# A hybrid retention/mLSTM layer step: third and fourth heads swapped, conditioning rows moved from the first mixer projection to the output projection, gates one head later

## The chip, the core and the metric

The kernel runs on one core of a Trainium2 chip. The metric is the device time of one execution in microseconds (us). A core has TensorE (PE) for matrix products, VectorE (DVE) and ScalarE (ACT) for elementwise work, GpSimd (POOL) for some more of it, and 16 DMA engines; the SyncE queue (SP) issues nearly all loads. Each engine works off its own queue strictly in order, and instructions wait on semaphores for other engines.

## What is computed

One layer over 384 tokens of width 2048 (128 context tokens and 256 latent tokens): adaptive layer norm, a mixer of four retention heads and four mLSTM heads, an output projection with a residual and post-norm, then a convolutional feed-forward block.

```python
sh1, sc1, g1, sh2, sc2, g2 = jnp.split(silu(c) @ w_mod + b_mod, 6)   # conditioning, context and latent
h = _ln(x) * (1.0 + sc1) + sh1
proj = h @ w_in                       # per head q, k, v and an output gate; 16 gate columns
gates = proj[..., off + 4 * M:] + b_gate        # input and forget gates of the mLSTM heads
ret_out = _ln(retention forward + backward) * gn_ret * silu(rg)       # 4 heads of 256
mlstm_out = sigmoid(mo) * _ln(mlstm forward + backward) * gn_mlstm    # 4 heads of 256
x = _ln(ALPHA * x + g1 * (concat(ret_out, mlstm_out) @ w_out)) * ln1_g + ln1_b
h = _ln(x) * (1.0 + sc2) + sh2
x = _ln(ALPHA * x + g2 * ffn(h)) * ln2_g + ln2_b
```

## The kernel before

Every large product is made to float32 accuracy out of three TensorE passes: a weight tile `raw` is split into a high part `hi` (ScalarE, line 117) and a low part `lo` (mostly VectorE, every sixth tile on GpSimd, line 118), and the products hi·hi, hi·lo and lo·hi are added up (lines 182 to 184 and 190 to 192). There are four `raw` buffers and three each of `hi` and `lo`, so a split can run at most about three weight tiles ahead of TensorE.

The mixer works head by head. Heads 0 and 1 of the retention are projected in a first phase, while the first parts of the conditioning are computed. The remaining six heads stand in the list `heads` at positions 2 to 7 (retention 2 and 3, mLSTM 0 to 3), and a loop over these positions projects each: `proj_a` for q and k (`psa`, four weight tiles each) and `proj_b` for v and the output gate (`psb`, eight weight tiles), so 16 weight tiles a head. After each weight tile `beside()` lets three generators go on by a number of steps that their `rate` sets:

- `behind`: the attention of the head two positions earlier (at position 7, of those at 5 and 6). Its products are `sc` (scores), `pm` (mLSTM decay rows), `num` (outputs), `cst_ps` or `rst_ps` (new states) and `mxp` (transposes into the rows `mixt`).
- `gating`, rate 0.5: the mLSTM gates (`cps`, `gsum`, `gsel`, `gcp` on TensorE; logarithms, scans and copies on VectorE, lines 547 to 555 and 594 to 642).
- `mods2`, rate 0.9: five blocks of conditioning rows. A block takes 16 loads `mraw` of 512 KB from `w_mod` (three buffers), two VectorE multiply-adds into `macc` for each (lines 283 and 286, so 32 a block), then TensorE sums over partitions (`modr`), the bias is added (`mbt`) and the row goes to memory. There is one `macc` buffer.

After the loop the first 512 columns of the output projection are begun (`pso`, seven weight tiles beside the attention of position 7), and finished with the two last rows of `mixt`, which that attention delivers; then come the other three column blocks.

The order in which the code is written only gives priorities: the framework's scheduler lists the instructions by its own timeline, and an instruction written later may stand earlier when its inputs are ready. PSUM tiles of the attentions, of the gates and of `modr` share three buffers (`pat`).

In what follows S2 to S7 are the stretches in which positions 2 to 7 are projected, and O is the one of the first output columns. Each begins with the first matmul of its `psa` (or `pso`) in TensorE's timeline.

Of the kernel before, what the change touches and what calls it, by code (L numbers as in the profile page):

```python
# [17 lines left out]
KT = D // P  # L18
# [5 lines left out]
NH = 4  # L24
# [58 lines left out]
def hybrid_step(ctx, tc, ca, cb, x_prompt, x_sample, state_ret, state_c, state_n, state_m, c, c_ctx,  # L83
# [29 lines left out]
    def transpose(out, in_, n=P):  # L113
        nc.tensor.transpose(out, in_, ident[:n, :n])
# [20 lines left out]
    def rows_bcast(dst, src_row, n):  # L135
        nc.gpsimd.dma_start(out=dst, in_=src_row.to_broadcast([P, n]))

    def weights(loads, n=1024, perm=False):
        raw = wraw.tile([P, 1024], F32, tag="raw", name="raw")
        for view, src in loads:  # L140
            nc.sync.dma_start(out=view(raw), in_=src)
        return split_weights(raw, n, perm)
# [19 lines left out]
    def weights_b(w2, k0, nk, cols):  # L162
        n = 512 // len(cols)
        loads = []
        for j, c0 in enumerate(cols):
            src = w2[k0 * P:(k0 + nk) * P, c0:c0 + n].rearrange("(k p) n -> p k n", p=P)
            loads.append((lambda r, j=j: r[:, :nk * 512].rearrange("p (k n) -> p k n", k=nk)[:, :, j * n:(j + 1) * n],
                          src))
        return weights(loads, nk * 512)
# [4 lines left out]
    def new_act(kt, src, eng=None):  # L174
        act_hi[kt] = acts.tile([P, T], F32R, tag=f"ah{kt}", name=f"ah{kt}")
        act_lo[kt] = acts.tile([P, T], F32R, tag=f"al{kt}", name=f"al{kt}")
        split(act_hi[kt], act_lo[kt], src, eng)
# [8 lines left out]
    def mm_b(ps, w, kk, ah, al, tt, start, stop, c0=0, n=512):  # L186
        hi, lo = w
        s = slice(kk * 512 + c0, kk * 512 + c0 + n)
        t = slice(tt * P, (tt + 1) * P)
        nc.tensor.matmul(ps, lhsT=ah[:, t], rhs=hi[:, s], start=start, stop=False)  # L190
        nc.tensor.matmul(ps, lhsT=ah[:, t], rhs=lo[:, s], start=False, stop=False)  # L191
        nc.tensor.matmul(ps, lhsT=al[:, t], rhs=hi[:, s], start=False, stop=stop)  # L192
# [3 lines left out]
    def rstd(out, var, n=1):  # L196
        v = small.tile([P, NT], F32, tag="veps", name="veps")
        nc.vector.tensor_scalar(out=v[:, :n], in0=var, scalar1=EPS, scalar2=None, op0=ALU.add)
        with tc.high_priority():
            mark["pow"] = nc.gpsimd.tensor_tensor(out=out, in0=v[:, :n], in1=mhalf[:, :n], op=ALU.pow).ins  # L200
# [118 lines left out]
    def chain(*gens):  # L319
        for g in gens:  # L320
            yield from g
# [66 lines left out]
    def part_b(ps, w, nk, k0, ks, ke):  # L388
        for kk in range(nk):
            kt = k0 + kk  # L390
            for tt in range(NT):
                mm_b(ps[tt], w, kk, act_hi[kt], act_lo[kt], tt, kt == ks, kt == ke)
# [26 lines left out]
    with ExitStack() as p0:  # L419
# [53 lines left out]
        for kt in range(KT):  # L473
            ps = pmm.tile([P, T], F32, tag="ps", name="xtp")
# [40 lines left out]
    with p1:  # L515
# [72 lines left out]
        def gates():  # L588
# [49 lines left out]
            for n, src in enumerate((ga, gem)):  # L638
                for d in range(2):
                    for tt in range(NT):  # L640
# [4 lines left out]
        gating = Stepper(gates(), 0.5)  # L645
# [3 lines left out]
        mods2 = Stepper(chain(mod_vector(2, pat, mp, raws2), mod_vector(3, pat, mp, raws2),  # L649
                              mod_vector(4, pat, mp, raws2, range(NV))), 0.9)  # L650
# [47 lines left out]
        def head_tail(hh, og, gn, h, last=False):  # L698
            st = small.tile([P, NT, 6], F32, tag="hst", name="hst")
            mv = small.tile([P, NT, 2], F32, tag="hmv", name="hmv")  # L700
            rs = small.tile([P, NT], F32, tag="hrs", name="hrs")
            for tt in range(NT):
                nc.vector.bn_stats(out=st[:, tt, :], in_=hh[:, tt, :])
                nc.vector.bn_aggr(out=mv[:, tt, :], in_=st[:, tt:tt + 1, :])
            rstd(rs, mv[:, :, 1], NT)
            for tt in range(NT):
                nc.vector.tensor_scalar(out=hh[:, tt, :], in0=hh[:, tt, :], scalar1=mv[:, tt, 0:1],
                                        scalar2=rs[:, tt:tt + 1], op0=ALU.subtract, op1=ALU.mult)
            g = gn[:, h * HD:(h + 1) * HD].unsqueeze(1).to_broadcast([P, NT, HD])
            if last:  # L710
                nc.vector.tensor_tensor(og, og, g, op=ALU.mult)
            else:
                nc.gpsimd.tensor_tensor(out=og, in0=og, in1=g, op=ALU.mult)
            nc.vector.tensor_tensor(hh, hh, og, op=ALU.mult)
# [22 lines left out]
        def mlstm_attn(h, q, k, vx, og):  # L737
# [3 lines left out]
            for d in range(2):  # L741
# [28 lines left out]
                i = d * 8 + h * 2  # L770
# [6 lines left out]
            hh = sb.tile([P, NT, HD], F32, tag="hh", name="hh", bufs=1)  # L777
            for tt in range(NT):
                for d in range(2):
                    ps = pat.tile([P, 257], F32, tag="ps", name="num")  # L780
# [22 lines left out]
                        nc.vector.scalar_tensor_tensor(out=hh[:, tt, :], in0=ps[:, 0:HD], scalar=dn,  # L803
                                                       in1=hh[:, tt, :], op0=ALU.mult, op1=ALU.add)
                yield
            head_tail(hh, og, gn_m[0], h, h == NH - 1)
            for d in range(2):
                st = sb.tile([P, 2, HD], F32, tag="st", name="st")
                for kd in range(2):
                    ps = pat.tile([P, 257], F32, tag="ps", name="cst_ps")  # L810
# [3 lines left out]
                    i = d * 8 + h * 2 + kd  # L814
# [21 lines left out]
        def ret_attn(h, q, k, vx, og):  # L836
# [62 lines left out]
            for fd in range(2):  # L899
                mix_columns(hh, 2 * h, fd)  # L900
                yield

        heads = [(ret_proj, ret_attn, h) for h in range(NH)] + [(mlstm_proj, mlstm_attn, h) for h in range(NH)]
        got = list(first)
        gn_m = []

        def attention(i):
            return heads[i][1](heads[i][2], *got[i])

        def new_acts(*kts):  # L910
            for kt in kts:
                new_act(kt, mixt[kt])

        for i in range(2, 8):
            if i == 6:
                gating.finish()
                gn_m.append(tab.tile([P, 1024], F32, tag="gn", name="gnm"))
                rows_bcast(gn_m[0], gn_mlstm.rearrange("a h v -> a (h v)"), 1024)
            last = i == 7
            behind[:] = [Stepper(chain(*[attention(j) for j in ((5, 6) if last else (i - 2,))]), 1.55 if last else 1.0)]  # L920
            got.append(heads[i][0](heads[i][2], [lambda j=j: new_acts(2 * j, 2 * j + 1) for j in range(5)] if last else ()))
            behind.pop().finish()
        mods2.finish()
        new_acts(*range(10, KT - 2))
        wo = w_out[0]
        pso = [pmm.tile([P, 512], F32, tag="ps", name="pso") for _ in range(NT)]
        attn = Stepper(attention(7), 1.75)
        attn.step()
        for k0 in range(0, KT - 2, 2):
            part_b(pso, weights_b(wo, k0, 2, (0,)), 2, k0, 0, KT - 1)  # L930
            attn.step()
        attn.finish()
        pn = pat.tile([16, P], F32, tag="ps", name="pn")
        transpose(pn, ncol)
        nrow = tab.tile([16, P], F32, name="nrow")
# [46 lines left out]
    with ExitStack() as p2:  # L982
# [2 lines left out]
        g1b = g1p.tile([P, 2, D], F32, name="g1b")  # L985
        l1g = g1p.tile([P, D], F32, name="l1g")
        l1b = g1p.tile([P, D], F32, name="l1b")
        for kt in range(KT - 2, KT):
            new_act(kt, mixt[kt])
        mixs.close()  # L990
        share_splits(0)
# [7 lines left out]
        def residual_loads(nb):  # L999
            s = slice(nb * 512, (nb + 1) * 512)  # L1000
            for tt in range(NT):
                nc.sync.dma_start(out=r[tt][:, s], in_=tok_rows(x_prompt, x_sample, tt)[:, s])
            for v in range(2):
                nc.sync.dma_start(out=g1b[:, v, s], in_=modrow[2, v:v + 1, s].to_broadcast([P, 512]))

        def w_out_block(nb):
            ps = pso if nb == 0 else [(pat if nb == 1 else pmm).tile([P, 512], F32, tag="ps", name="pso")
                                      for _ in range(NT)]
            for k0 in range(KT - 2 if nb == 0 else 0, KT, 2):
                part_b(ps, weights_b(wo, k0, 2, (nb * 512,)), 2, k0, 0, KT - 1)  # L1010
                if nb > 0:
                    mods4.step()
                if k0 == (10 if nb else KT - 2):
                    residual_loads(nb)
                if nb == 2 and k0 == 14:
                    residual_loads(3)
                if nb == 1 and k0 == 8:
                    mod_from_rows(3, KT, pat, sb2, "sh2", 0.0)
                if nb == 2 and k0 == 6:
                    rows_bcast(l1g, ln1_g, D)  # L1020
                    rows_bcast(l1b, ln1_b, D)
                if nb == 2 and k0 == 8:
                    mod_from_rows(4, 8 * NV, pat, sb2, "sc2", 1.0)
            return ps

        for nb in range(3):
            ps = w_out_block(nb)
            for tt in range(NT):
                residual(sb2, g1b, tt, nb, ps[tt], True, True)
# [3 lines left out]
        ps = [pmm.tile([P, 512], F32, tag="ps", name="pso") for _ in range(NT)]  # L1033
# [67 lines left out]
        for i in range(KT + 2):  # L1101
# [6 lines left out]
            kt = i - 2  # L1108
# [109 lines left out]
    for nb in range(4):  # L1218
        for k0 in (39, 41):
# [3 lines left out]
            i = len(ws)  # L1223
# [58 lines left out]
```

## Time and profile before

| | us |
|---|---|
| median of 3 runs (2072.29 to 2074.78) | 2074.51 |
| the profiled execution | 2073.23 |
| its span, first to last instruction | 2071.4 |
| TensorE busy in the span | 1989.1 (96%) |
| VectorE busy | 1231.2 (59%) |
| ScalarE busy | 690.3 (33%) |
| GpSimd busy | 238.4 (12%) |
| S2 to S7 and O, 227.4 to 814.9 | 587.5 |

Busy time of TensorE is that of overlapping records, so a stretch without idle time may still hold matmuls that are paced by a lower clock; the granted clock is listed beside it. A number in square brackets behind a row of a timeline is the idle time of the engine just before it, with the instruction that ended it.

### The profile page before, as it was taken

The numbers are of one execution on the slowest core, as the hardware profiler recorded it, in microseconds if no ns is written. First come the engines' busy times: TensorE is split into PE (matmuls) and PEld (weight loads), VectorE is DVE, ScalarE is ACT, GpSimd is POOL, SyncE is SP. The second block draws the span as 40 slices with busy tenths as digits, with TensorE's granted clock in tenths as the row PEclk, the third lists the DMA queues.
The fourth block names the chain that finished last, engine by engine and source line by source line (L and its number), as shares of the span: only waits on it lengthen the run. The fifth ranks groups of instructions, "written<-read, shape, count | busy, mean of one in ns | idle before, by whom it ended". The sixth has DMA issues, their size and how long they took to land.

```text
span 2071.4 us, 26316 instructions
## 1 busy us (share of the span) xinstructions
PE 1989.1 (96%) x10233; PEld 1752.3 (85%) x10233; DVE 1231.2 (59%) x1791; ACT 690.3 (33%) x1050; POOL 238.4 (12%) x226
## 2 busy tenths in 40 slices
PE   6999899999989999998999999999999999999995
PEld 4677878899888876777999889999889998999984
DVE  4655699987868754477944333477434444444478
ACT  4223333333333443235333333333222332233331
POOL 0001353231212111012000000000000000000004
PEclk9999999999999999998999999999999999999998
DMA  9895976887886435834744334466334444434342
GB/s 346 259 308 167 167 189 182 257 211 214 199 175 213 147 111 209 282 109 140 251 124 125 125 127 123 125 193 195 123 122 126 125 136 153 123 110 143 113 153 102
DMA packets 260637, 352.30 MB, mean 170 GB/s; under 512 B 16143, under 2 KB 200784, under 8 KB 259360
## 3 DMA queue, kind: packets, MB, share of 16 engines
q1 hardware_dynamic: 256240, 340.08, 55.3%
q0 software_dynamic: 4272, 10.54, 1.5%
q8 instruction: 80, 1.31, 0.3%
q14 instruction: 45, 0.37, 0.1%
HBM read 343.16 MB, written 7.41 MB: 169 GB/s over the span
## 4 chain that ended last, share of the span: by engine, by line
PE 81%; DVE 7%; DMA 5%; issue 3%; POOL 1%; SPq 1%; ACT 1%; POOLq 0%; DVEq 0%; ACTq 0%
PE psu L182 11%; PE psu L184 11%; PE psu L183 11%; PE psd L192 5%; PE psd L190 5%; PE psd L191 5%; PE psa L182 3%; PE psa L184 3%; PE psa L183 3%; DMA mraw<-in_w_mod 3%; PE psb L191 3%; DVE macc L286 3%; PE psb L192 3%; PE psb L190 3%; PE pso L190 2%
## 5 line engine op out<-in xcount | busy, mean ns | idle before, releaser
L118 DVE TENSOR_TENSOR lo<-raw,hi 128x1024 fp32r<-128x1024 f32 (+4 forms) x443 | 479.9, 1090 | 541.6 <-ACT hi L117 541.2
L117 ACT CAST hi<-raw 128x1024 fp32r<-128x1024 f32 (+4 forms) x473 | 435.1, 929 | 977.9 <-PE psu L183 358.8
L183 PE MATMUL psu<-al,hi 128*128 128x384 f32 x1376 | 467.4, 340 | 0.0
L184 PE MATMUL psu<-ah,lo 128*128 128x384 f32 x1376 | 464.1, 339 | 2.7 <-DVE lo L118 2.7
L182 PE MATMUL psu<-ah,hi 128*128 128x384 f32 x1376 | 466.6, 340 | 0.0
L286 DVE SCALAR_TENSOR_TENSOR macc<-mraw,ct,macc 128x1024 f32<-128x1024 f32 x210 | 287.6, 1405 | 17.4 <-DMA mraw<-in_w_mod 17.4
L184 PEld LDWEIGHTS psu<-ah,lo 128*128 128x128 f32 x1376 | 258.9, 188 | 3.0 <-DVE lo L118 3.0
L182 PEld LDWEIGHTS psu<-ah,hi 128*128 128x128 f32 x1376 | 258.8, 188 | 1.9 <-ACT hi L117 0.8
L183 PEld LDWEIGHTS psu<-al,hi 128*128 128x128 f32 x1376 | 259.2, 188 | 0.1
L192 PE MATMUL psd<-hi,fal 128*128 128x512 f32 (+1 forms) x484 | 191.3, 395 | 0.0
L191 PE MATMUL psd<-lo,fah 128*128 128x512 f32 (+1 forms) x484 | 189.5, 392 | 0.0
L190 PE MATMUL psd<-hi,fah 128*128 128x512 f32 (+1 forms) x484 | 187.7, 392 | 0.0
L184 PE MATMUL psa<-ah,lo 128*128 128x384 f32 x512 | 176.9, 347 | 7.5 <-DVE lo L118 7.4
L182 PE MATMUL psa<-ah,hi 128*128 128x384 f32 x512 | 179.7, 356 | 1.7 <-ACT hi L117 1.7
L183 PE MATMUL psa<-al,hi 128*128 128x384 f32 x512 | 176.9, 346 | 0.0
L191 PE MATMUL psb<-lo,ah 128*128 128x512 f32 x384 | 155.2, 404 | 5.5 <-DVE lo L118 5.5
L192 PE MATMUL psb<-hi,al 128*128 128x512 f32 x384 | 153.5, 400 | 0.0
L190 PE MATMUL psb<-hi,ah 128*128 128x512 f32 x384 | 151.7, 408 | 1.7 <-ACT hi L117 1.7
L182 PEld LDWEIGHTS psa<-ah,hi 128*128 128x128 f32 x512 | 98.1, 192 | 15.5 <-issue 8.8
L191 PEld LDWEIGHTS psd<-lo,fah 128*128 128x128 f32 x484 | 90.8, 188 | 22.4
L192 PEld LDWEIGHTS psd<-hi,fal 128*128 128x128 f32 x484 | 90.9, 188 | 21.6
L190 PEld LDWEIGHTS psd<-hi,fah 128*128 128x128 f32 x484 | 90.9, 188 | 20.9
(301 smaller groups left out, 2240.7 us busy)
## 6 DMA issues: line engine op xcount, KB each, us to landing
raw<-in_w_up SPq DMA_DIRECT2D x168, 512.0 KB, 3.8
mraw<-in_w_mod SPq DMA_DIRECT2D x112, 512.0 KB, 5.0
raw<-in_w_down SPq DMA_DIRECT2D x84, 512.0 KB, 3.6
raw<-in_w_in SPq DMA_DIRECT2D x128, 256.0 KB, 4.6
raw<-in_w_in SPq DMA_DIRECT2D x52, 512.0 KB, 6.7
wm<-in_w_mod SPq DMA_DIRECT2D x20, 1024.0 KB, 8.9
raw<-in_w_out SPq DMA_DIRECT2D x32, 512.0 KB, 4.0
wm<-in_w_mod SPq DMA_DIRECT2D x16, 768.0 KB, 7.4
```

Source lines behind the costliest of these rows:

```text
L117: nc.scalar.copy(dst_hi, src)
L118: mark["lo"] = (eng or nc.vector).tensor_tensor(out=dst_lo, in0=src, in1=dst_hi.bitcast(F32), op=ALU.subtract).ins
L182: nc.tensor.matmul(ps, lhsT=hi[:, s], rhs=ah, start=start, stop=False)
L183: nc.tensor.matmul(ps, lhsT=hi[:, s], rhs=al, start=False, stop=False)
L184: nc.tensor.matmul(ps, lhsT=lo[:, s], rhs=ah, start=False, stop=stop)
L190: nc.tensor.matmul(ps, lhsT=ah[:, t], rhs=hi[:, s], start=start, stop=False)
L191: nc.tensor.matmul(ps, lhsT=ah[:, t], rhs=lo[:, s], start=False, stop=False)
L192: nc.tensor.matmul(ps, lhsT=al[:, t], rhs=hi[:, s], start=False, stop=stop)
L286: nc.vector.scalar_tensor_tensor(out=acc[:, v, :], in0=raw, scalar=ct[:, kt, v:v + 1], in1=acc[:, v, :], op0=ALU.mult, op1=ALU.add)
```

## The change

Three things are changed. The heads stand in the order 0, 1, 3, 2 for both kinds, so that the last head to be attended writes rows 12 and 13 of `mixt`, and the output projection leaves these two for last. The rate of `mods2` is 0 at position 2 and 0.94 from position 3 on, and what is left of it steps on beside the seven weight tiles of O. The rate of `gating` is 0.6 at position 3 and 0 elsewhere.

```diff
-            head_tail(hh, og, gn_m[0], h, h == NH - 1)
+            head_tail(hh, og, gn_m[0], h, h == turn[-1])
...
-        heads = [(ret_proj, ret_attn, h) for h in range(NH)] + [(mlstm_proj, mlstm_attn, h) for h in range(NH)]
+        turn = (0, 1, 3, 2)
+        heads = [(ret_proj, ret_attn, h) for h in turn] + [(mlstm_proj, mlstm_attn, h) for h in turn]
...
         for i in range(2, 8):
+            mods2.rate = 0.0 if i == 2 else 0.94
+            gating.rate = 0.6 if i == 3 else 0.0
...
-        mods2.finish()
-        new_acts(*range(10, KT - 2))
+        new_acts(10, 11, 14, 15)
...
-        for k0 in range(0, KT - 2, 2):
-            part_b(pso, weights_b(wo, k0, 2, (0,)), 2, k0, 0, KT - 1)
+        for k0 in (0, 2, 4, 6, 8, 10, 14):
+            part_b(pso, weights_b(wo, k0, 2, (0,)), 2, k0, 0, 13)
+            mods2.step()
             attn.step()
         attn.finish()
+        mods2.finish()
...
-        for kt in range(KT - 2, KT):
+        for kt in (12, 13):
             new_act(kt, mixt[kt])
...
-            for k0 in range(KT - 2 if nb == 0 else 0, KT, 2):
-                part_b(ps, weights_b(wo, k0, 2, (nb * 512,)), 2, k0, 0, KT - 1)
+            for k0 in (12,) if nb == 0 else range(0, KT, 2):
+                part_b(ps, weights_b(wo, k0, 2, (nb * 512,)), 2, k0, 0, KT - 1 if nb else 13)
```

What the scheduler makes of it is seen in the order of the instructions.

First, VectorE near the start of S2. `macc<-mraw` are the conditioning rows, `lo<-raw` halves of split weight tiles, `rt` and `k` the rotation of the keys of the first two heads, `tz` the decay table of an attention. Before:

```order
L840 SCALAR_TENSOR_TENSOR tz<-cs,lgb_2129,tz 128x384
L283 TENSOR_SCALAR macc<-mraw,ct 128x1024 x2
L843 TENSOR_TENSOR tz<-tz,cst 128x128
L286 SCALAR_TENSOR_TENSOR macc<-mraw,ct,macc 128x1024 x2
L118 TENSOR_TENSOR lo<-raw,hi 128x4x128
L844 TENSOR_SCALAR tz<-tz 128x384
L567 TENSOR_TENSOR rt_2148<-k,cs 128x256
L118 TENSOR_TENSOR lo<-raw,hi 128x4x128
```

The same place after:

```order
L840 SCALAR_TENSOR_TENSOR tz<-cs,lgb_2129,tz 128x384
L843 TENSOR_TENSOR tz<-tz,cst 128x128
L844 TENSOR_SCALAR tz<-tz 128x384
L118 TENSOR_TENSOR lo<-raw,hi 128x4x128
L567 TENSOR_TENSOR rt_2148<-k,cs 128x256
L118 TENSOR_TENSOR lo<-raw,hi 128x4x128
L568 TENSOR_TENSOR rt_2149<-k,cs 128x256
L570 TENSOR_TENSOR k<-k,cs 128x256
L569 TENSOR_TENSOR k<-k,cs 128x256
L283 TENSOR_SCALAR macc<-mraw,ct 128x1024 x2
```

The first rows of `macc` no longer stand ahead of this weight tile. They have not left S2, though: all 32 of the first block still stand on VectorE ahead of the first weight tile of S3, since nothing before them there keeps them back. What does leave S2 are the gates. The first block's `modr`, which before came in S3, now comes in S4, and with one `macc` buffer no `macc` stands in S3 at all. The last block's last 14 `macc` and its `modr` stand in O.

Second, VectorE in S6, where the attention of the first mLSTM head begins (`wt<-pm` are its decay weights). Before:

```order
L286 SCALAR_TENSOR_TENSOR macc<-mraw,ct,macc 128x1024 x6
L118 TENSOR_TENSOR lo<-raw,hi 128x1024
L286 SCALAR_TENSOR_TENSOR macc<-mraw,ct,macc 128x1024 x2
L118 TENSOR_TENSOR lo<-raw,hi 128x1024
L286 SCALAR_TENSOR_TENSOR macc<-mraw,ct,macc 128x1024 x3
L751 TENSOR_TENSOR wt_4998<-pm,cs 128x256
L751 TENSOR_TENSOR wt_4998<-pm,cs 128x128 x2
L286 SCALAR_TENSOR_TENSOR macc<-mraw,ct,macc 128x1024
```

After, at the same attention:

```order
L286 SCALAR_TENSOR_TENSOR macc<-mraw,ct,macc 128x1024 x4
L118 TENSOR_TENSOR lo<-raw,hi 128x1024 x2
L751 TENSOR_TENSOR wt_4932<-pm,cs 128x256
L751 TENSOR_TENSOR wt_4932<-pm,cs 128x128 x2
L118 TENSOR_TENSOR lo<-raw,hi 128x1024
L763 SCALAR_TENSOR_TENSOR wt_4932<-sc_4890,wt_4932 128x256
```

The `macc` right ahead of and among the `wt` are gone. Instead ten `macc` of the next block stand further on in S6, between the first and the second `hh` that adds both directions of this attention. In S7 likewise no `macc` stands any more among the `wt` of the attention of position 5.

Third, TensorE in O, at the second `pm` of the last attention (that of position 7). Before, 32 rows of `pso` stand between it and its `num`:

```order
L192 MATMUL pso<-hi,al_6496 128x512
L190 MATMUL pso<-hi,ah_6508 128x512
L191 MATMUL pso<-lo,ah_6508 128x512
L192 MATMUL pso<-hi,al_6509 128x512
L743 MATMUL pm<-gnegm,cst 128x384
L190 MATMUL pso<-hi,ah_6508 128x512
L191 MATMUL pso<-lo,ah_6508 128x512
L192 MATMUL pso<-hi,al_6509 128x512
```

After:

```order
L190 MATMUL pso<-hi,ah_6494 128x512
L191 MATMUL pso<-lo,ah_6494 128x512
L192 MATMUL pso<-hi,al_6495 128x512
L743 MATMUL pm<-gnegm,cst 128x384
L795 MATMUL num<-vx,wt_6541 128x257
L795 MATMUL num<-vx,wt_6565 128x257
L795 MATMUL num<-vx,wt_6541 128x257
L795 MATMUL num<-c_6560,qs 128x257 x2
```

The `num` of the last attention now follow its second `pm` at once. Those of the attention before it, which before stood at the end of S7, stand in O, and the last attention's `sc` come after three quarters of O's `pso`. The orders of the feed-forward block and of what follows it differ by little.

More of the change, by code (lines that the diff above doesn't have):

```diff
@@ L1008, in w_out_block @@
                                       for _ in range(NT)]
-            for k0 in range(KT - 2 if nb == 0 else 0, KT, 2):
-                part_b(ps, weights_b(wo, k0, 2, (nb * 512,)), 2, k0, 0, KT - 1)
+            for k0 in (12,) if nb == 0 else range(0, KT, 2):
+                part_b(ps, weights_b(wo, k0, 2, (nb * 512,)), 2, k0, 0, KT - 1 if nb else 13)
                 if nb > 0:
                     mods4.step()
-                if k0 == (10 if nb else KT - 2):
+                if k0 == (10 if nb else 12):
                     residual_loads(nb)
```

## The prediction

> **What bounds the kernel now.** I read the page's busy times and chain first, then busy times by stage, then in each stage the waits of TensorE.
>
> ```profile
> span 2071.4 us, 26316 instructions
> PE 1989.1 (96%) x10233; PEld 1752.3 (85%) x10233; DVE 1231.2 (59%) x1791; ACT 690.3 (33%) x1050; POOL 238.4 (12%) x226
> PE 81%; DVE 7%; DMA 5%; issue 3%; POOL 1%; SPq 1%; ACT 1%; POOLq 0%; DVEq 0%; ACTq 0%
> ```
>
> TensorE sets the end: 96% busy and 81% of the chain. No edit here takes matmuls away, so all there is to gain is its waits and the slow clock behind them. The busy times by stage (columns: length, then busy and count of PE, PEld, DVE, ACT, POOL, granted clock, DMA share, GB/s) show where these lie; the two timeline rows are the first matmuls of S2 and of what follows O.
>
> ```profile
> 227.40:325.90 98.50, 87.41 (x403) 73.23 (x402) 90.47 (x115) 31.69 (x55) 46.50 (x28) 0.95 0.82 201
> 325.90:408.40 82.50, 82.13 (x417) 71.80 (x416) 76.97 (x92) 28.99 (x53) 25.26 (x24) 1.00 0.73 213
> 408.40:489.10 80.70, 80.70 (x408) 71.73 (x407) 68.17 (x81) 29.24 (x42) 22.49 (x19) 1.00 0.81 220
> 489.10:566.30 77.20, 77.20 (x389) 68.57 (x388) 57.21 (x68) 27.58 (x40) 17.34 (x18) 1.00 0.74 194
> 566.30:658.50 92.20, 85.97 (x409) 74.36 (x408) 72.16 (x107) 33.14 (x57) 16.62 (x17) 0.94 0.76 188
> 658.50:758.00 99.50, 96.09 (x454) 82.53 (x453) 67.66 (x136) 44.89 (x87) 20.11 (x19) 0.97 0.45 145
> 758.00:814.90 56.90, 53.35 (x230) 42.22 (x229) 27.48 (x73) 23.69 (x52) 10.42 (x11) 0.97 0.42 143
> 227.41 0.34 PE L182 MATMUL psa<-ah,hi 128*128 128x384 f32 x1
> 814.93 0.86 PE L190 MATMUL pso<-hi,ah 128*128 128x512 f32 x3
> ```
>
> TensorE idles 11.1 us in S2, 6.2 in S6, 3.4 in S7, 3.6 in O and 0.4 elsewhere: 24.7. The clock costs length times what it lacks: 4.9, 5.5, 3.0 and 1.7, together 15.1. So about 40 of the 587.5 us are stalls, 16 of them in S2, where VectorE is 92% busy. S3 to S5 have next to none.
>
> **S2, gates gone.** The waits at its start, and VectorE's work there:
>
> ```profile
> 239.49 1.42 DVE L283 TENSOR_SCALAR macc<-mraw,ct 128x1024 f32<-128x1024 f32 x2 [6.95 <-DMA mraw<-in_w_mod]
> 243.78 0.68 DVE L118 TENSOR_TENSOR lo<-raw,hi 128x512 fp32r<-128x512 f32 x1
> 244.52 0.45 PE L184 MATMUL psa<-ah,lo 128*128 128x384 f32 x1 [3.87 <-DVE lo L118]
> L621 DVE TENSOR_TENSOR_SCAN gb<-n0o,gf 4x128 f32<-4x128 f32 (+1 forms) x3 | 3.5, 1198 | 0.0
> L595 DVE COPY n0c<-cps 128x16 f32<-128x16 f32 x1 | 0.2, 156 | 0.0
> 227.40:325.90 98.50, 0.00 (x0) 0.00 (x0) 44.50 (x32) 0.95 0.82 201
> 325.90:408.40 82.50, 1.06 (x8) 0.16 (x8) 44.90 (x32) 1.00 0.73 213
> 658.50:758.00 99.50, 1.06 (x8) 0.16 (x8) 20.08 (x15) 0.97 0.45 145
> 758.00:814.90 56.90, 0.00 (x0) 0.00 (x0) 0.00 (x0) 0.97 0.42 143
> ```
>
> VectorE stands still for 6.95 us behind a conditioning row that has not landed, with the `lo` that TensorE needs behind it in the queue. In the new order that `lo` comes first, which lifts this one wait; the next `lo` stands behind the rows instead, and their loads are now issued behind the state loads and one more weight tile. I give that wait no gain of its own. The last four rows are the `macc` alone, in S2, S3, S7 and O: 44.5 us of VectorE in S2 are conditioning rows, and by the order these stay. The gates go: twelve groups, the first and the last shown, 13.6 us. From 239.5 to 325.9 VectorE is full (86.4 us); without 13.6 it needs 72.8, so S2 ends at 312.3 at best, 13.6 earlier. TensorE alone would allow 98.5 - 16.0 = 82.5, so VectorE stays the bound. The loads speak against the whole of it: 98.5 us at 201 GB/s are 19.8 MB, and the best stage, S4, has 220 GB/s, at which they take 90.0, a gain of 8.5. Between 13.6 and 8.5, both near rows of this stage, I take -10.5. Bounds: 0, if the loads keep to 201 GB/s, and -16, if every stall goes.
>
> A rule speaks against this term, too:
>
> ```profile
> 228.24 2.01 POOL L713 TENSOR_TENSOR og<-og,gnr 128x768 f32<-128x768 f32 x1 [10.23 <-ACT og L577]
> 228.47 2.06 DVE L568 TENSOR_TENSOR rt<-q,cs 128x256 f32<-128x256 f32 x1
> L568 DVE TENSOR_TENSOR rt<-k,cs 128x256 f32<-128x256 f32 x2 | 0.8, 413 | 0.0
> ```
>
> The same operation took 0.41 us on `k` and 2.06 us on `q`, where it ended just after GpSimd's. The Trainium skill (SBUF — State Buffer, section "SBUF: two separate sides") says that a VectorE operation with two SBUF inputs and a GpSimd operation exclude each other for a whole instruction; this row agrees. By that rule part of the gates' 13.6 us is waiting for GpSimd, whose 46.5 us stay in S2, and would pass to other instructions; if a quarter of it is such waiting, VectorE's gain is 10.2 instead of 13.6, the middle with 8.5 is -9.4, and the sum would be -13. The sum here goes without it.
>
> **S3, gates come.** VectorE has 77.0 us, of them 44.9 `macc`, which leave, and the gates' 13.6 arrive: far from full. Their matmuls (`gsum`, `gsel`, `cps`) come in place of one `modr` (1.06 in the row above). TensorE's order leaves most of three q/k tiles and thirteen `num` between `gsum` and the first `gsel`, so the chain of logarithms between is covered; if that cover fails, TensorE stands still for some of it. I take +1, bounds -1 and +5. The `macc` that leave S3 are spread over S4 to S7 and O, at 0.94 instead of 0.9 a tile: S4 and S5 have 12 and 20 us of VectorE free, and take as much as before or some seven rows more. I cost them at 0; the load side of it is a rival below.
>
> **S6 and S7.**
>
> ```profile
> 586.34 3.67 DVE L286 SCALAR_TENSOR_TENSOR macc<-mraw,ct,macc 128x1024 f32<-128x1024 f32 x3 [3.40 <-DMA mraw<-in_w_mod]
> 593.73 1.64 PE L743 MATMUL pm<-gnegm,cst 4*128 4x384 f32 x2 [6.03 <-DVE wk L757]
> 681.74 0.45 PE L184 MATMUL psa<-ah,lo 128*128 128x384 f32 x1 [2.32 <-DVE lo L118]
> 687.11 0.91 PE L743 MATMUL pm<-gnegm,cst 4*128 4x384 f32 x2 [1.09 <-DVE wk L757]
> L286 DVE SCALAR_TENSOR_TENSOR macc<-mraw,ct,macc x210: 1245/1276/3426, 241.4 to 1431.4; 128x1024 f32<-128x1024 f32 x105
> ```
>
> In S6 VectorE waits for rows that are late, the decay weights and `wk` wait behind them, and TensorE 6.03 us for `wk`; in S7 two such waits, 3.41 us. In the new order no `macc` stands there. That frees up to 6.2 + 5.5 = 11.7 in S6 and 6.4 in S7. Late next in S6 are the ten `macc` between the two `hh`: ten at the median 1.28 are 12.8 us, in which `num` runs out of PSUM buffers. TensorE has the last eleven `num` and some weight matmuls to do meanwhile; I take 4 us of wait and 2 of clock, so -6 (bounds -11.7 and +3: none of the new wait, or all of it on top of a clock loss as now). In S7 18 rows now stand in its second half, beside matmuls of both attentions; 2 us back, so -4.5 (bounds -6.4 and +2).
>
> **O, the cover of the last attention.**
>
> ```profile
> 786.89 0.91 PE L743 MATMUL pm<-gnegm,cst 4*128 4x384 f32 x2
> 787.38 1.22 DVE L118 TENSOR_TENSOR lo<-raw,hi 128x1024 fp32r<-128x1024 f32 x1 [2.40 <-ACT hi L117]
> 788.52 0.81 DVE L751 TENSOR_TENSOR wt<-pm,cs 128x128 f32<-128x128 f32 x3
> 791.19 0.28 DVE L763 SCALAR_TENSOR_TENSOR wt<-sc,wt 128x128 f32<-128x128 f32 x1
> 808.31 1.19 PE L114 MATMUL mxp<-cst,hh 128*128 128x128 f32 x6 [3.09 <-DVE hh L714]
> 810.87 0.63 PE L190 MATMUL pso<-hi,ah 128*128 128x512 f32 x1
> 811.30 0.63 PE L191 MATMUL pso<-lo,ah 128*128 128x512 f32 x1
> 812.36 0.39 PE L191 MATMUL pso<-lo,ah 128*128 128x512 f32 x1
> ```
>
> From the second `pm` to the last decay weight VectorE and ScalarE take 791.5 - 787.8 = 3.7 us, or near it; before, `pso` matmuls ran over it, now TensorE stands still. The wait of 3.09 us before `mxp` stays. After it the matmuls come 0.43 us apart (810.87 to 811.30) and later 0.23 (812.36 on), so short waits cost clock as well: +4 for the wait, +2 for the clock, +6. The 14 `macc` (14 x 1.28 = 17.9 us) fit beside 27.5 of 56.9 us of VectorE; the last `modr` falls in the wait before the last `pso`. Bounds 0 (the order's extra wait overlaps the chain that waits anyhow) and +14 (the rows delay the chain by most of their 17.9 us). The sixteen `num` moved from S7 to O add as much there as they take away. The Trainium skill (TensorE: Matmul & The Clock Gate, section "HAM oscillation — how this bites in real kernels") puts the loss of clock at gaps above 3.4 us; by it the term would be +4. The trace differs, with 3.09 us enough.
>
> The swap by itself moves no work: rows 14 and 15 are ready where 12 and 13 were. It costs 0; behind O nothing but a few neighbours in the order changes, 0 +/- 2.
>
> **The sum.** -10.5 + 1 - 6 - 4.5 + 6 = -14 us. Against the profiled execution (2073.23, of which 2071.4 span) that is 2059.2; the median of the runs is 1.3 above it, so 2060.5 is the forecast, 0.7% faster. A difference of 0.2%, 4.1 us, is about what can be told from none.
>
> **Rivals.** (1) S2 does not shorten. The words of the change say that the rows leave it, the order says they do not; if loads at 201 GB/s and not VectorE's gates set it, the -10.5 is 0: -3.5, 2071. For it: DMA share 0.82 with a wait of 6.95 us for a row. Against: VectorE shows no other large wait in 90.5 busy us. (2) Slower: loads become the bound in S4 to S7. In these the `macc` go from 98 to 114 (18 of the last block remain in S7), eight loads of 512 KB, 4.2 MB, 19 us at 220 GB/s. If all of it lands on TensorE: -14 + 19 = +5, 2079.5. It decides from where the DMA share nears 1; as stages the shares are 0.81, 0.74, 0.76 and 0.45, which speaks against it, but the 3.40 us wait in S6 shows that stretches are there already. (3) Every stall in S2, S6 and S7 goes: -16 + 1 - 11.7 - 6.4 + 6 = -27, 2047.5; ten `macc` among the `hh` speak against it.
>
> **Chances.** The forecast with its own bounds (2051 to 2069) 0.70, rival 1 0.15, rival 2 0.11, rival 3 0.04. Rival 1 lies at the edge of what can be told: 0.03 of it counts as faster, 0.12 as same. So faster 0.77, same 0.12, slower 0.11. The range 2049 to 2072 takes in the forecast's bounds and rival 1, and leaves out the other two.
>
> **What would show it.** S2 should be near 88 us with VectorE still the busiest and no gate in it; S3 near 83.5 with no `macc`; the wait of `pm` in S6 gone and S6 near 86, with a new wait at `num`; S7 and O together, 156.4 before, near 158; in O a wait of about 4 us between the second `pm` and `num`. It is wrong if S2 stays above 94, if `lo` or `num` wait behind rows with a DMA as their releaser in S4 to S7, or if the chain in O takes more than 10 us beyond today's.

## The result, and the profile after

The changed kernel takes 2062.22 us (median of 4 runs, 2059.26 to 2066.21) against 2074.45 for the kernel before, a ratio of 0.9944 with a 95% interval of 0.9925 to 0.9964: 0.6% faster, 1.7 us above the forecast of 2060.5 and inside its range. The sum came out near although several of its terms did not, and the experiments below give the credit to other causes than the prediction did.

The page of the changed kernel's profiled execution, which at 2066.21 us is the slowest of its four:

```profile
span 2064.4 us, 26334 instructions
PE 1988.4 (96%) x10233; PEld 1752.6 (85%) x10233; DVE 1231.4 (60%) x1791; ACT 694.1 (34%) x1052; POOL 233.0 (11%) x226
PE 82%; DVE 8%; DMA 3%; issue 3%; POOL 1%; SPq 1%; ACT 1%; POOLq 0%; DVEq 0%; ACTq 0%
```

TensorE still sets the end; the share of DMA in the chain fell from 5% to 3%. The stages S2 to S7 and O (columns as in the prediction's table):

```profile
229.70:314.10 84.40, 80.32 (x391) 71.44 (x391) 78.51 (x96) 27.57 (x51) 33.91 (x27) 0.98 0.75 204
314.10:405.10 91.00, 85.84 (x418) 73.06 (x417) 49.42 (x78) 33.26 (x57) 20.22 (x20) 0.96 0.74 131
405.10:485.20 80.10, 80.10 (x404) 71.16 (x403) 70.39 (x82) 29.39 (x42) 22.57 (x19) 1.00 0.81 220
485.20:564.40 79.20, 79.20 (x400) 70.33 (x399) 64.08 (x77) 27.74 (x40) 17.91 (x18) 1.00 0.70 216
564.40:645.40 81.00, 81.00 (x399) 70.53 (x398) 65.15 (x102) 32.84 (x55) 16.70 (x17) 1.00 0.72 200
645.40:736.90 91.50, 89.96 (x433) 76.60 (x432) 79.37 (x126) 43.96 (x81) 25.09 (x20) 0.98 0.78 191
736.90:808.20 71.30, 63.84 (x264) 48.69 (x264) 51.70 (x111) 28.73 (x62) 16.95 (x16) 0.93 0.52 174
```

S2 is 14.1 us shorter, S6 11.2, S7 8.0; S3 is 8.5 longer, S5 2, O 14.4. The stretch ahead of S2, which the change does not touch, happened to be 2.3 longer in this execution. Work changed places between S7 and O: 26 `num` went (58 and 38 before, 32 and 64 after), 6.2 us in S7. The two stages together are 6.4 us longer.

In S2 VectorE, busy for 78.5 us, is no longer ahead of TensorE with 80.3, and it waits 5.3 us for conditioning rows that have not landed.

S3 was the surprise. Its start in the timeline, VectorE, ScalarE and TensorE:

```profile
306.38 2.48 DVE L286 SCALAR_TENSOR_TENSOR macc<-mraw,ct,macc 128x1024 f32<-128x1024 f32 x2 [1.77 <-DMA mraw<-in_w_mod]
312.25 1.14 ACT L117 CAST hi<-raw 128x512 fp32r<-128x512 f32 x2 [6.04 <-DMA raw<-in_w_in]
313.49 4.03 DVE L286 SCALAR_TENSOR_TENSOR macc<-mraw,ct,macc 128x1024 f32<-128x1024 f32 x2 [3.49 <-DMA mraw<-in_w_mod]
317.45 4.10 DVE L118 TENSOR_TENSOR lo<-raw,hi 128x512 fp32r<-128x512 f32 x4
319.80 0.69 PE L184 MATMUL psa<-ah,lo 128*128 128x384 f32 x1 [5.16 <-DVE lo L118]
```

The first weight tile of S3 lands so late that ScalarE stands still for 6.04 us, and the last two rows of S2 come later still: VectorE waits 3.49 us for them with the split `lo` behind them, and TensorE waits 5.16 us for that `lo`, where it waited 0.37 us in all of S3 before. The rest of S3's growth, 3.7 us, is busy time of TensorE, which has the gates' matmuls to do (busy us, mean ns):

```profile
L612 PE MATMUL gsel<-lgs,cst 16*4 16x384 f32 x4 | 1.6, 481 | 0.0
L612 PE MATMUL gsel<-gts,cst 16*4 16x384 f32 x4 | 1.6, 481 | 0.0
L600 PE MATMUL gsum<-gpt,cst 32*16 32x384 f32 x2 | 0.8, 487 | 0.0
L114 PE MATMUL cps<-cst,cqr 16*128 16x16 f32 x3 | 0.4, 215 | 0.0
L114 PE MATMUL cps<-cst,n0o 16*128 16x16 f32 x1 | 0.2, 208 | 0.0
```

These matmuls take 4.6 us, in S2 before and in S3 now. In what follows a row is one `macc` instruction, two to a load `mraw`, and a row is late when its load is. The `macc` by stage (S2, S3 and O) lie where the order had put them: the rows left S3, not S2.

```profile
229.71:314.13 84.42, 0.00 (x0) 0.00 (x0) 41.77 (x31) 0.98 0.75 204
314.13:405.09 90.96, 0.00 (x0) 0.00 (x0) 3.39 (x2) 0.96 0.74 131
736.95:808.20 71.25, 1.94 (x8) 0.20 (x8) 19.78 (x14) 0.93 0.52 174
```

In O the foretold wait stands behind the second decay matrix:

```profile
781.12 0.91 PE L743 MATMUL pm<-gnegm,cst 4*128 4x384 f32 x2
782.06 0.82 DVE L751 TENSOR_TENSOR wt<-pm,cs 128x128 f32<-128x128 f32 x3 [2.19 <-PE pm L743]
782.80 1.22 DVE L118 TENSOR_TENSOR lo<-raw,hi 128x1024 fp32r<-128x1024 f32 x1
783.93 0.62 DVE L763 SCALAR_TENSOR_TENSOR wt<-sc,wt 128x128 f32<-128x128 f32 x2
784.60 3.16 PE L795 MATMUL num<-vx,wt 128*128 128x257 f32 x6 [2.58 <-DVE wt L763]
```

No row stands between `pm` and the last `wt`, only the chain itself and one split. Behind the wait of 2.58 us the granted clock was 0.56 from 784.6 to 792.0 us, so the `num` there run at about half pace: six take 3.16 us, where four take 1.03 later on.

### The profile page after: what moved, and what is told of

Read it like the earlier page. It is cut to its first block, busy times and chain, and to the rows that moved or that the text cites. A ratio compares the mean times of both kernels' runs of the same rounds, so it can differ in the third digit from the quotient of the medians.

```text
span 2064.4 us, 26334 instructions
## 1 busy us (share of the span) xinstructions
PE 1988.4 (96%) x10233; PEld 1752.6 (85%) x10233; DVE 1231.4 (60%) x1791; ACT 694.1 (34%) x1052; POOL 233.0 (11%) x226
## 4 chain that ended last, share of the span: by engine, by line
PE 82%; DVE 8%; DMA 3%; issue 3%; POOL 1%; SPq 1%; ACT 1%; POOLq 0%; DVEq 0%; ACTq 0%
PE psu L184 12%; PE psu L182 12%; PE psu L183 12%; PE psd L192 5%; PE psd L191 5%; PE psd L190 5%; PE psa L182 4%; PE psa L184 4%; PE psa L183 4%; PE psb L190 3%; PE psb L191 3%; PE psb L192 3%; DVE macc L286 3%; DMA mraw<-in_w_mod 2%; PE modps L255 2%
```

## The experiments

The first theory was that of the prediction: the gates leave a full VectorE in S2, the rows leave the decay weights of S6, and the swap is nothing. The lengths of the stages of all kernels in their profiled executions, in us (the last column is the span from the start of O to the end):

```
kernel                       S2    S3    S4    S5    S6    S7     from O on
before                      98.5  82.5  80.7  77.3  92.2  99.4   1313.4
changed                     84.4  91.0  80.1  79.2  81.0  91.5   1327.5
changed, once more          84.1  91.4  80.1  79.2  81.0  91.7   1326.3
gates alone                 90.3  84.8  86.8  77.3  90.6 101.6   1313.1
rows alone                  95.9  79.5  80.0  79.2  81.0  88.8   1326.5
swap alone                  93.4  85.5  80.7  77.3  84.2 101.0   1313.2
rows and gates, no swap     85.3  85.7  80.1  79.2  81.0  88.8   1327.0
the same, once more         85.3  85.0  80.1  79.2  81.0  87.7   1325.3
rows and swap, no gates     92.6  84.7  80.0  79.2  81.0  90.8   1326.5
before, other columns       93.2  82.8  80.7  77.3  82.5  99.2   1312.9
changed, other columns      83.6  85.7  80.1  79.2  81.0  87.7   1326.5
rows end in S7              86.3  85.3  79.2  80.7  89.3  83.4   1333.7
rows early                  88.0  85.5  81.7  78.8  85.1  94.6   1310.5
rows early, second          85.7  85.2  82.6  81.0  86.2  97.7   1312.3
```

**Gates alone.** The kernel before with one line in the loop over positions:

```diff
         for i in range(2, 8):
+            gating.rate = 0.6 if i == 3 else 0.0
```

> The kernel before with the gates one head later and nothing else: conditioning rows run at their old rate and finish ahead of O, heads unswapped. Theory: VectorE is full in S2 and the gates' 13.6 us are what S2 can lose, so S2 shortens by 10 to 14 us (98.5 to 84.5-88.5); S6 keeps its wait of about 6 us at the decay weights because rows still stand ahead of them, and O keeps its 57 us; in all 2074.5 - 12 = 2062 to 2065 us, about the whole of what the change brought. Rival (the rows carry the gain): S2 stays within 3 us of 98.5 and the time within 4 us of 2074.5.

Measured: 2073.65 us against 2073.07, ratio 1.0002 (0.9993 to 1.0011). The theory's 12 us did not come; the time is the rival's, though S2 did shorten. The stage rows of S2 and S4, and two waits of TensorE:

```profile
229.16:319.43 90.27, 82.48 (x392) 72.02 (x391) 80.85 (x99) 27.65 (x50) 35.85 (x28) 0.96 0.87 208
404.23:491.01 86.78, 83.85 (x418) 74.22 (x417) 79.05 (x94) 31.13 (x45) 24.04 (x21) 0.98 0.80 213
```

```profile
417.79 0.34 PE L114 MATMUL gcp<-cst,gi 4*128 4x4 f32 x3 [2.93 <-ACT gi L632]
595.12 1.64 PE L743 MATMUL pm<-gnegm,cst 4*128 4x384 f32 x2 [5.96 <-DVE wk L757]
```

S2 is 8.2 us shorter, but 4.6 of that are the gates' matmuls, and only 3.3 are waits (TensorE idles 7.8 us there instead of 11.1). S4 pays 6.1: the end of the gates stands there beside 34 rows, and TensorE waits 2.93 us for `gi`. S3 and S7 are 2.3 and 2.2 longer, and S6 keeps its wait.

**Rows alone.** The kernel before with

```diff
         for i in range(2, 8):
+            mods2.rate = 0.0 if i == 2 else 0.94
...
-        mods2.finish()
         new_acts(*range(10, KT - 2))
...
             part_b(pso, weights_b(wo, k0, 2, (0,)), 2, k0, 0, KT - 1)
+            mods2.step()
             attn.step()
         attn.finish()
+        mods2.finish()
```

> The kernel before with the conditioning rows at rate 0 in S2 and 0.94 from S3 on, going on into O, and nothing else: gates and heads as before. Theory: the order keeps 29 rows in S2 whatever the rate says, with the gates beside them, so S2 stays at 95 to 100 us; S6 loses its 11 us because no row stands ahead of the decay weights, O with S7 gains 6; in all 2074.5 - 11 + 6 - 1 = 2068.5, range 2066 to 2071. Rival (the rows carry the gain): the time is that of the changed kernel, 2062.

Measured: 2061.70 us, ratio 0.9938 (0.9926 to 0.9951): the rival's number. S6 is 11.2 us shorter, as the theory had it; S7 with all behind it is 2.5 longer where 6 were expected, and S2 and S3 together lose 5.6 where 1 was expected: 2.6 in S2, and 3.0 in S3, which the `modr` and its rows leave.

**Swap alone.** The kernel before with the two lists of heads in the order 0, 1, 3, 2, and in O the tiles 0 to 11, 14, 15 ahead of 12, 13.

> The kernel before with the third and fourth heads swapped and O's tiles taken as 0 to 11, 14, 15 and then 12, 13; rates as before. Theory: the swap moves no work, 2074.5 within 4 us, every stage within 1.5 us of before except for moved matmuls. Rival (the swap releases something): more than 4 us faster, with a stage that shows it.

Measured: 2064.68 us, ratio 0.9958 (0.9946 to 0.9971). The edit that was costed at 0 brings 8.4 us: S2 is 5.1 shorter and S6 8.0, while S3 is 3.0 longer and S7 1.6. Two stretches of the DMA engines show why, first before (the last two columns are the DMA share and GB/s):

```profile
206.00:230.00 24.00, 24.00 (x122) 21.17 (x121) 14.37 (x27) 10.51 (x15) 7.01 (x5) 1.00 1.03 121
302.00:344.00 42.00, 42.00 (x209) 33.48 (x208) 36.54 (x54) 16.75 (x32) 9.91 (x10) 1.00 0.62 180
```

Then with the swap alone:

```profile
206.00:230.00 24.00, 24.00 (x121) 21.12 (x120) 14.23 (x27) 10.52 (x15) 6.67 (x5) 1.00 0.60 148
302.00:344.00 42.00, 41.74 (x212) 33.80 (x211) 37.56 (x55) 15.86 (x31) 10.03 (x12) 1.00 1.00 177
```

Before, the engines are full at 121 GB/s just ahead of S2, where the weights of the third retention head load; a window of 8 us at 398 us, as full, moves 306. With the swap the same place moves 148 GB/s at a share of 0.60, and the full stretch stands ahead of S3 instead, where that head now loads. The mLSTM heads show the same at 546 us, just ahead of S6, though less sharply (share 1.02 at 196 GB/s, with the swap 0.81 at 255), and at 630 us. The second theory: loads of the third head's columns are slow, and the rows, which share the queue, come late behind them.

**Rows and gates without the swap.** The two edits above together.

> The changed kernel without the swap: gates at position 3, rows from S3 into O, heads unswapped. Theory: as the changed kernel, 2062 within 4 us, S2 near 85, S6 near 81, S7 with O near 163. Rival (the swap is part of the gain): more than 4 us slower than the changed kernel. A second question: whether S3 again shows 8 us more than before (a wait of about 5 us of TensorE for a split behind late rows at its start); theory, that it belongs to rows whose loads are issued late in S2, says it does, the rival, that it was one execution's bad luck with a slow stretch of the DMA engines, says S3 is then near 83.5.

Measured: 2055.76 us, ratio 0.9917 (0.9904 to 0.9931), and 2053.36 in a second comparison (below). By the ratios it is 6 to 7 us faster than the changed kernel, which neither the theory nor the rival had: S3 is 85.7, of which 4.6 are the gates, and the wait at its start is 1.45 us instead of 5.16. On top of the other two edits the swap costs what its slow loads do to S3 and S7; on top of the rows alone it costs nothing (0.9938 for the rows, 0.9940 for rows and swap, below).

**Other columns.** Two kernels, before and changed, in which the third head of each kind reads the fourth head's columns of `w_in`, in loads of the same number and size. What they compute is no longer the layer; only their times are used.

```diff
-        return [base + 1024 * i + h * HD for i in range(4)]
+        return [base + 1024 * i + (3 if h == 2 else h) * HD for i in range(4)]
```

> The kernel before, where the third head of each kind reads the fourth head's columns of w_in (its results are then not the reference's; every instruction and the size of every load stay). Theory (the stretch in which the DMA engines are full at about 100 GB/s belongs to the third head's columns, and before's waits in S2 and S6 stand behind it): no such stretch at 204-232 us and 546-576 us, S2 5 or more us shorter, S6 8 to 11 shorter, 2073 - 15 = 2058, range 2055 to 2064. Rival (the stretch belongs to the place in the program, or to what else is loaded there): stretch and stages as before, 2073 within 4.

> The changed kernel with the same edit: the third head of each kind, now fourth in turn, reads the fourth head's columns. Theory: of S3's 8.5 us, 4.6 are matmuls of the gates that moved there and 5 the wait behind the third head's slow loads, so S3 goes from 91.0 to 85.5, S7 from 91.5 to 89, no stretch at 300-345 and 630-678 us; 2061 - 7 = 2054, range 2051 to 2057. Rival (S3's wait comes from rows and gates together, whatever the loads): S3 stays at 91 and the time within 3 us of the changed kernel.

Measured: 2058.73 us from before (ratio 0.9929, 0.9916 to 0.9941) and 2052.26 from the changed kernel (0.9899, 0.9885 to 0.9912; the changed kernel beside them 0.9945). The loads issued from 206 to 230 us, S2's first (count, KB each, median us to landing), before:

```profile
raw<-in_w_in SPq DMA_DIRECT2D x5, 512.0 KB, 9.3
mraw<-in_w_mod SPq DMA_DIRECT2D x3, 512.0 KB, 15.1
```

and before with other columns, with the stretch itself:

```profile
raw<-in_w_in SPq DMA_DIRECT2D x5, 512.0 KB, 5.2
mraw<-in_w_mod SPq DMA_DIRECT2D x3, 512.0 KB, 7.9
```

```profile
206.00:230.00 24.00, 24.00 (x120) 20.98 (x120) 13.65 (x27) 10.45 (x15) 6.08 (x5) 1.00 0.58 145
```

The stretch ahead of S6, in before and in before with other columns:

```profile
546.00:570.00 24.00, 23.80 (x109) 19.47 (x108) 20.76 (x16) 8.90 (x14) 4.44 (x2) 1.00 1.02 196
546.00:570.00 24.00, 24.00 (x116) 20.58 (x115) 20.53 (x16) 9.03 (x14) 5.14 (x2) 1.00 0.71 249
```

Ahead of S2 the same load takes 5.2 us instead of 9.3, and a load of conditioning rows in the same queue 7.9 instead of 15.1. That is worth 14.8 us in before (S2 5.3, S6 9.7) and 10.1 in the changed kernel (S3 5.3, S7 3.8). Both times came within 2 us of what was expected: the slow columns stand behind S6's wait and behind what the swap does. S6's wait needs both, rows ahead of the decay weights and rows that are late: with other columns S6 is 82.5 us and TensorE does not wait, with its rows in place.

**The changed kernel once more.**

> The changed kernel once more, beside the three above. Theory: the wait of about 5 us at the start of S3 and the slow stretches at 300-345 and 630-678 us come again, and the time is 2061 within 2, some 5 us above the kernel without the swap. Rival (they were one execution's): S3 near 86 and the time near 2056.

Measured: 2062.33 us, ratio 0.9945 (0.9932 to 0.9959). The stages agree within 0.4 us and the wait in S3 is there again, 5.69 us. It is no accident of one execution.

**Rows and swap, gates back.** The changed kernel without the line `gating.rate = 0.6 if i == 3 else 0.0`.

> The changed kernel with the gates back where they were (heads swapped, rows from position 3 into O). Theory: the gates' own 4.6 us of matmuls go back from S3 to S2, and about 4 us of waits come back to S2, so S2 96, S3 about 86 with the wait of 5 us at its start still there, since it stands behind the late loads and not behind the gates; 2061.5 + 4 = 2065, range 2062 to 2068. Rival (S3's wait needs the gates beside the late loads): S3 falls to 80 and the time is 2059 to 2061, below the changed kernel.

Measured: 2062.04 us, ratio 0.9940 (0.9926 to 0.9953), no other than the changed kernel's. The theory expected 2065 and the rival at most 2061. S2 and S3 in it, then two waits of VectorE and the one wait of TensorE in S3:

```profile
228.23:320.87 92.64, 87.66 (x409) 72.72 (x408) 85.67 (x113) 32.84 (x56) 59.18 (x27) 0.96 0.68 187
320.87:405.59 84.72, 82.65 (x402) 73.30 (x401) 37.77 (x61) 28.07 (x51) 21.90 (x20) 0.96 0.72 140
```

S3 lies between the two expectations, with the wait behind late rows gone:

```profile
309.41 1.28 DVE L286 SCALAR_TENSOR_TENSOR macc<-mraw,ct,macc 128x1024 f32<-128x1024 f32 x1 [1.03 <-DMA mraw<-in_w_mod]
315.64 1.28 DVE L286 SCALAR_TENSOR_TENSOR macc<-mraw,ct,macc 128x1024 f32<-128x1024 f32 x1 [0.80 <-DMA mraw<-in_w_mod]
328.30 0.35 PE L114 MATMUL gcp<-cst,gf 4*128 4x4 f32 x3 [2.07 <-DVE gf L624]
```

With the gates in place VectorE reaches the late rows later and waits 1.03 and 0.80 us for them; without the gates it is there early and waits 1.77 and 3.49. With less to do VectorE waits longer for the same rows, and S2 and S3 together take 177.3 us with the gates in S2 and 175.4 with them in S3.

**Rows that end in S7.** The kernel with rows and gates, no swap, with the rates

```diff
-            mods2.rate = 0.0 if i == 2 else 0.94
+            mods2.rate = {2: 0.0, 3: 1.4}.get(i, 0.92)
```

and `mods2.finish()` ahead of O again, as before the change.

> The changed kernel without the swap, with rows at 1.4 in position 3 and 0.92 from 4 on, so that they end ahead of O: S7 has 32 of them instead of 24, O none instead of 14. Theory (O's 7 us beyond moved work are the rows that share VectorE with the last decay weights, and the wait of 2.6 us there): S7 and O together go from 160 to 156, the time from 2055.8 to 2052. Rival (that wait is TensorE's own order in O, and S7 now pays for eight more rows): S7 and O together stay at 160 or grow, 2055.8 to 2059.

Measured: 2068.81 us, ratio 0.9975 (0.9966 to 0.9985), 12 to 13 us above the kernel that it was made from; neither expectation has that. VectorE in S6, and TensorE's waits in S6 and O:

```profile
571.66 1.28 DVE L286 SCALAR_TENSOR_TENSOR macc<-mraw,ct,macc 128x1024 f32<-128x1024 f32 x1 [2.26 <-DMA mraw<-in_w_mod]
574.00 4.87 DVE L286 SCALAR_TENSOR_TENSOR macc<-mraw,ct,macc 128x1024 f32<-128x1024 f32 x4
584.80 0.91 PE L743 MATMUL pm<-gnegm,cst 4*128 4x384 f32 x2 [1.82 <-DVE wk L757]
786.27 1.23 PE L795 MATMUL num<-vx,wt 128*128 128x257 f32 x2 [3.68 <-DVE wt L763]
```

Two things follow. With other rates the order has rows ahead of the decay weights in S6 again, in the slow stretch of the third mLSTM head, and S6 is back at 89.3 us, 8.3 of the loss. And O has no row left, yet its wait at the last `wt` is 3.68 us: so that wait does not need rows in O; it goes with TensorE's order there.

**Rows early.** As the last, but with rates chosen so that S6 has no row ahead of its last decay weight and O's order of matmuls is that of before:

```diff
+            mods2.rate = {2: 0.4, 3: 1.7, 4: 0.8}.get(i, 0.85)
```

> The changed kernel without the swap, with the rows earlier: rates 0.4, 1.7 and 0.8 in positions 2 to 4, 0.85 after, so that S2 to S7 have 32, 18, 39, 35, 26 and 10 of them and O none; in S6 none stands between its second pair of rows and the last decay weight, and in O output matmuls stand between the second decay matrix and its num again, as before the change. Theory: a row costs something only where it stands ahead of what TensorE waits for, so O with S7 loses the 6.4 us that the change put there and S6 stays at 81; 2055.8 - 6 = 2050, range 2047 to 2053. Rival (VectorE or the loads become the bound in S4 and S5, with 39 and 35 rows instead of 32 and 28): S4 and S5 take 5 to 10 us more, 2055 to 2060.

A second kernel has the rates 0, 2.0 and 0.85.

> The same with rates 0, 2.0 and 0.85: 32, 14, 39, 39, 24 and 12 rows in S2 to S7 and none in O, S6 and O ordered as in the kernel with rates 0.4, 1.7 and 0.8. Theory: as that one, 2050 within 3. Rival: S4 and S5, with 39 rows each, take 5 us more or above, 2055 to 2062.

> The changed kernel without the swap once more, beside the two above: 2055.8 within 2, S2 85, S3 86, S6 81, S7 89.

Measured beside each other: 2055.38 (ratio 0.9914, 0.9901 to 0.9927), 2060.29 (0.9937, 0.9923 to 0.9952), and 2053.36 for the kernel with rows and gates without the swap (0.9910, 0.9895 to 0.9925). The stages S6 and S7 with the rates 0.4, 1.7, 0.8, and the wait in S6:

```profile
562.21:647.36 85.15, 82.21 (x405) 71.06 (x404) 71.77 (x106) 32.96 (x57) 19.16 (x18) 1.00 0.87 207
647.36:741.94 94.58, 94.58 (x463) 81.20 (x462) 66.69 (x140) 46.07 (x90) 21.41 (x21) 1.00 0.42 135
```

```profile
596.90 1.13 PE L795 MATMUL num<-vx,wt 128*128 128x257 f32 x4 [2.01 <-ACT dn L797]
```

S7 and all behind it gain 10.7 us (94.6 + 1310.5 against 88.8 + 1327.0), more than the 6.4 that the change had put there, and TensorE does not wait at all in S7, nor at `wt` in O, where the order is that of before. Of it S6 takes back 4.1, now behind `dn`, S2 2.7 and S4 1.6, and the stretch ahead of S2 was 2 us longer. By the medians nothing is left. The second kernel lies in the time range of its rival, but S4 and S5 are only 2.5 and 1.8 us longer than without the early rows; S6 takes 5.2 more, the stretch ahead of S2 4.6 more in that execution, and S7 with all behind it 5.8 less. Its runs spread from 2055.89 to 2064.42, and no run shows why. No version that computes the layer is faster than the change without its swap.

## Why the prediction was right, and where it was not

The total (-14 forecast, -12.2 measured) is the sum of errors of both signs, and that it came within 1.7 us is luck. By the profiles S2 to O are 9.0 us shorter (8.7 in the second profile of the changed kernel), where the terms had 14; the rest of the 12.2 lies ahead of S2, behind O and in the spread of the runs. The bounds of the terms, added up, reach from -37 to +26; the range that held is much narrower and was not worked out from them.

- **S2, -10.5; it is -14.1.** 4.6 of that are the gates' matmuls, which only moved; the true gain is about 9.5. The term took its gain from VectorE's busy time and gave the wait for the first `lo` (3.87 us, behind a late row) "no gain of its own". Here are the other large wait of TensorE in S2 before, then the first `lo` with the gates alone, then with the rows alone:

```profile
295.44 0.79 PE L191 MATMUL psb<-lo,ah 128*128 128x512 f32 x1 [4.29 <-DVE lo L118]
245.74 0.69 PE L184 MATMUL psa<-ah,lo 128*128 128x384 f32 x1 [3.35 <-DVE lo L118]
250.06 0.44 PE L184 MATMUL psa<-ah,lo 128*128 128x384 f32 x1 [0.21 <-DVE lo L118]
```

The gates alone cut the first of these to 1.65 us and leave the wait at the start of S2. The rows take that one away by their order. With the swap alone, or with other columns, it is gone too, and there the rows still stand ahead of the `lo` but land in time. Swap, rows and gates each take 3 to 5 us of S2's 11.1 us of waits, and together 7.0. For the whole kernel the gates are worth little: alone, moving them brings nothing, and beside swap and rows it brings nothing either; on top of the rows, without the swap, it brings some 4 us (0.9938 to 0.9917, with intervals that overlap a little).
- **S3, +1, bounds -1 and +5; it is +8.5.** This is the step that failed. The gates' matmuls came "in place of one `modr`", but they are 4.6 us against 1.1, on the engine that sets the end, and the term asked only whether the chain between them was covered; TensorE's busy time in S3 grew by 3.7 us. The other 4.8 are waiting, 5.16 at the start against 0.37 in all before. The prediction had seen the pattern in before's S2 (6.95 us for a row, the `lo` behind it) and in the change of order, but not that the swap carries the slow loads to S3.
- **S6, -6; it is -11.2.** All of the wait and the slow clock behind it went: that is 9.7 us, by the 82.5 us of before with other columns. The rest is work that now stands in S5 and S7 (four `sc` and six `mxp`). The new wait at `num`, costed at 4 us and its clock, did not come: TensorE has no wait in S6.
- **S7 and O, +1.5 together; they are +6.4.** In S7 waits at `lo` of 1.5 us are left of 3.4, behind rows that VectorE waits for by up to 1.50 us; a `lo` behind late rows was one of the signs named for a wrong forecast, and it showed in this small size. In O the wait of 2.58 us at `wt` is there as foretold, with 1.09 more at `ncol` and a lower clock (0.93 for 0.97). The moved `num` (26, where the prediction counted sixteen) were to add in O what they take from S7, but they add 9.2 us and take 6.2, as part of them runs in the slow clock behind that wait. The last `modr`, which was costed at 0, takes 1.94.
- **The swap, 0.** Alone it is worth -8.4 us; on top of the other two it costs 6 to 7. It was costed by its instructions, and they are indeed the same; what changes is which bytes load when.

Rival 1, that loads and not VectorE's gates set S2, had a part of the mechanism and the wrong size: not all loads at 201 GB/s, but those of one head. The views that would have told it were there: short windows show full engines at 121 GB/s just ahead of S2 and at 196 just ahead of S6, the two stages with the largest waits, and the third head of a kind stands in both.

## What to carry to other kernels

Price a moved step first on the engine that sets the end: its own matmuls go along, and a stage that shortens by them alone has gained nothing. Where an engine is full, look for what it would wait on if it had less to do; only a run with the work taken out shows whether the time or only the name of the idle changes. And read DMA share and GB/s together in short windows: a full share at a low rate (here 121 GB/s, where another full window had 306) marks a place from which to keep other loads away, by order, before any compute is moved.

## What the runs showed of the hardware

Loads of one and the same shape run at different speeds by the columns they read. The third of four heads (columns 512 to 767 of each block of 1024 in `w_in`) fills the DMA engines at 121 GB/s, where the fourth head's in its place need a share of 0.58 for 145. All heads have the same row pitch, 8208 floats or 32,832 bytes, so 128 rows are 4 MiB and 8 KiB apart. The Trainium skill (DMA: Bandwidth & Descriptors, section "Latency and other measured facts") measured 103 GB/s for copies whose rows lie 4 MiB apart from partition to partition, 207 at 512 KiB and 214 at 4 MiB and 4 KiB, and supposes, unverified, that HBM channels alias. The rate here is near its slow figure, but the case differs: rows of neighbouring partitions lie 32,832 bytes apart, and a rule on the pitch alone does not tell one head from the next. No run here shows the cause, and whether a padded layout would cure it was not tried.

A wait of TensorE as short as 2.58 us was followed by matmuls at about half pace, with a granted clock of 0.56 over the next 7.4 us (the changed kernel, O).
